# Latent attention's queries in 12 products with transferred rotary parts, and weights loaded four chunks ahead

## The chip, the cores and the metric

The kernel runs on one core of a Trainium2 chip. The metric is the device time of one execution in microseconds. Before the change it is 2968.56 us (median of 3 runs, 2968.51 to 2968.79).

## The reference

A two-layer encoder on 512 tokens of width 1024, all in float32. A layer is a half-step SwiGLU, a mixing block with three kinds of attention, a second half-step SwiGLU, and a gated per-layer input. The change touches the first kind of attention only, multi-head latent attention with 16 heads:

```python
q = (rms_norm(c_q, q_norm) @ w_uq).reshape(b, s, MLA_HEADS, MLA_NOPE + MLA_ROPE)   # 384 -> 16 x (64 + 32)
q_nope = q[..., :MLA_NOPE]
q_rope = apply_rope(q[..., MLA_NOPE:], cos[:, None, :], sin[:, None, :])
kv = (rms_norm(c_kv, kv_norm) @ w_ukv).reshape(b, s, MLA_HEADS, MLA_NOPE + MLA_V)
k_nope, v = kv[..., :MLA_NOPE], kv[..., MLA_NOPE:]
k_rope = apply_rope(k_rope, cos, sin)                       # one for all heads
logits = (einsum('bqhd,bkhd->bhqk', qn, k_nope) + einsum('bqhr,bkr->bhqk', qr, k_rope)) * 96 ** -0.5
```

`apply_rope` splits the 32 numbers into halves x1 and x2 of 16 and gives [x1 cos - x2 sin, x2 cos + x1 sin], here called the turned part. The 64 numbers without rotation are a head's own part.

## The kernel before, in words

**Arithmetic.** Each float32 matrix is split into a high part, cast to a reduced format (fp32r), and a low part, the difference. A product takes three matmuls: high by high, low by high, high by low (`mm3`, L224 is the matmul's line). `split` (L235, L236) makes the parts of an activation: a cast on ScalarE, a subtraction on VectorE.

**Tiles.** Activations lie as tiles of 128 features by 512 tokens. They come from one ring of 62 tiles (`SLOTS`). A product goes to a PSUM bank; of the eight banks three ("a") serve projections and five ("s") the heads' logits and outputs.

**Weights.** All weights are laid out on the host as chunks of 128 x 1024 in the order of use (`_chunk`). `Weights.get` (L128) names a chunk, orders the split of chunks up to two ahead (`SPLIT_AHEAD`), and the load of chunks up to five ahead (`LOAD_AHEAD`, L72). Loads go out on SyncE's queue (L88) into four raw buffers. A chunk is cast on ScalarE (L101), and its low part is made by VectorE (L107) or, in the heads' stage (`by_load`, from L1192), by a negated copy on ScalarE (L104) and an accumulating transfer from the raw buffer that GpSimd issues (L105). The raw buffer is free after that. The split parts have three buffers.

**The mixing block** (`mix`) projects the normalised input to the query latent (three tiles, `cq`), the key and value latent (two tiles, `ckv`) and the rotary key. The key tiles `KA` exist three times for two heads each (`KSETS` = 3): one half of such a tile holds the head's own 64 key rows, the other half 64 rows with the 32 turned key rows twice. Then 40 heads follow each other: 16 latent, 8 differential, 16 windowed. A head's steps are logits (`Mla.logits`, L1001), softmax, transposes, values.

**The order of the work.** Each head's own work is written out in order. The projections that later heads need stand in a queue (`Filler`, L136), sorted by the head at which they are due; `pace` works out how many matmuls per head are to be done, over the whole queue ahead, and `pump` takes that many between a head's steps. What a head needs is forced beforehand (`need`). Pair j (`mla_pair`, L844, the queries and own keys of heads 2j and 2j+1) may start at head 2(j-2), when the key tiles of pair j-3 are free, and is due before head 2j. Pair 0 and the first values are forced before head 0 (L1190). The framework's scheduler then orders each engine's instructions; every engine, SyncE among them, works through its own list in order.

**A pair before the change.** The queries of each head take a product of their own of 128 rows: 64 own rows, the 32 rotary rows, and the same 32 with their halves exchanged. One VectorE multiplication by a table (`trig`, L850) scales the own rows, multiplies the rotary rows by cosine and the exchanged ones by sine. The tile is split. The two products of the rotary rows are added only in the logits' matmul, where both meet the same turned key rows. A pair is thus 9 + 9 matmuls for the queries and 6 for the keys (24 units in the queue), and four tiles of the ring stay until its heads are done.

Of the kernel before, what the change touches and what calls it, by code (L numbers as in the profile page):

```python
# [12 lines left out]
F32 = mybir.dt.float32  # L13
F32R = mybir.dt.float32r
AF = mybir.ActivationFunctionType
ALU = mybir.AluOpType
# [4 lines left out]
P = 128  # L21
D = 1024
KT = D // P
T = 512
# [4 lines left out]
NH = 16  # L29
NHD = 8  # L30
QL = 384
KVL = 256
SCALE_A = 96 ** -0.5
# [34 lines left out]
class Weights:  # L68

    LOAD_AHEAD = 5  # L72
    SPLIT_AHEAD = 2

    def __init__(self, nc, pool, wall):
# [52 lines left out]
    def get(self, *keys):  # L128
        first = self.claim(*keys)[0]
        self.halve(first + max(1 + self.SPLIT_AHEAD, len(keys)))  # L130
        self.load(first + 1 + self.LOAD_AHEAD)
        out = [self.parts.pop(first + i) for i in range(len(keys))]
# [50 lines left out]
def encoder_kernel(ctx: ExitStack, tc: tile.TileContext, ins, out):  # L183
    nc = tc.nc
# [22 lines left out]
    def S(name, dt=F32):  # L207
        return sb.tile([P, 512], dt, tag="slot", name=name, bufs=SLOTS)
# [4 lines left out]
    turn = [0]  # L213

    def PS(name, kind=None):


        if kind is None:
            kind = CYCLE[turn[0] % len(CYCLE)]
            turn[0] += 1  # L220
        return psp.tile([P, 512], F32, tag="ps" + kind, name=name, bufs=BANKS[kind])
# [4 lines left out]
    def mm3(ps, lh, ll, rh, rl, start, stop):  # L226
        mm(ps, lh, rh, start, False)
        mm(ps, ll, rh, False, False)
        mm(ps, lh, rl, False, stop)

    def split(src, name, tile=None):

        tile = tile or S
        hi, lo = tile(name + "h", F32R), tile(name + "l", F32R)
        nc.scalar.copy(hi, src)  # L235
        nc.vector.tensor_sub(lo, src, hi.bitcast(F32))  # L236
        return hi, lo
# [12 lines left out]
    t = S("one")  # L250
# [11 lines left out]
    for l in range(L):  # L262
        for i, at in enumerate((S_F1, S_F2)):
            s = slice(l * 8 + 4 * i, l * 8 + 4 * i + 4)
# [147 lines left out]
    def proj(ps, w, z, i0=0, n=KT, cols=P):  # L412

        wh, wl = w
        for k in range(n):
            c = slice(i0 + k * cols, i0 + k * cols + cols)
            mm3(ps, wh[:, c], wl[:, c], z[k][0], z[k][1], k == 0, k == n - 1)
            if side:
                side.popleft()()
            yield 3  # L420
# [301 lines left out]
    def mix(l, prep, p2):  # L722
        name = f"m{l}"
# [3 lines left out]
        def kept(nm, dt=F32):  # L727
            return stage.tile([P, 512], dt, tag="kept", name=f"{name}{nm}", bufs=17)
# [16 lines left out]
        for d in range(KT):  # L745
            if d % 4 == 0:
                w = W.get(("ple_proj", l, d // 4))
            ps = PS(f"{name}pp{d // 4}{d % 4}")
# [12 lines left out]
        trig = [kept(f"trig{i}") for i in range(3)]  # L761
# [45 lines left out]
        cq, ckv, got = end_q(), [], {}  # L807
# [13 lines left out]
                ckv.extend(end_kv())  # L821

        merged = [None] * KT

        def mla_v(g):
            wh, wl = W.get(("mla_v", l, g))
            vs = [S(f"{name}va{g}_{tb}", F32R) for tb in range(TB)]
            for tb in range(TB):
                ps = PS(f"{name}va{g}_{tb}", "a")[:, 0:256]
                ts = slice(tb * P, (tb + 1) * P)  # L830
                for k in range(2):
                    w = slice(k * 256, (k + 1) * 256)
                    mm(ps, ckv[k][0][:, ts], wh[:, w], k == 0, False)
                    mm(ps, ckv[k][1][:, ts], wh[:, w], False, False)
                    mm(ps, ckv[k][0][:, ts], wl[:, w], False, k == 1)

                v = vs[tb].rearrange("p (g x c) -> p g x c", x=4, c=64)
                src = ps.rearrange("p (g e c) -> p g e c", e=2, c=64)
                nc.scalar.copy(v[:, :, 0::3, :], src)
                nc.vector.tensor_sub(v[:, :, 1:3, :], src, v[:, :, 0::3, :].bitcast(F32))  # L840
                yield 3
            got["va", g] = vs

        def mla_pair(j):  # L844
            wh, wl = W.get(("mla_pair", l, j))
            for e in range(2):
                ps = PS(f"{name}qa{j}{e}", "a")
                yield from proj(ps, (wh, wl), cq, i0=e * 384, n=3)
                t = S(f"{name}qa{j}{e}")
                nc.vector.tensor_mul(t, ps, trig[e])  # L850
                got["qa", 2 * j + e] = split(t, f"{name}qa{j}{e}")
            ps = PS(f"{name}kap{j}", "a")
            yield from proj(ps, (wh, wl), ckv, i0=768, n=2)
            for e in range(2):
                r = slice(0, 64) if e == 0 else slice(64, 128)
                kh, kl = KA[j % KSETS][e]
                nc.scalar.copy(kh[r], ps[r])
                nc.vector.tensor_sub(kl[r], ps[r], kh[r].bitcast(F32))

        halves = (slice(0, 64), slice(64, 128))  # L860

        def q_pair(key, at, j):

# [305 lines left out]


        A0, C0, B0, END = 0, NH, NH + NHD, 2 * NH + NHD
        work = [(A0 + 2 * j - 1, ("pair", j), 24, mla_pair(j)) for j in range(8)]
        work += [(A0 + 4 * g, ("va", g), 12, mla_v(g)) for g in range(4)]
        work += [(A0 + 2 * j + 1, ("ga", j), 24, gate("ga", C_GA, j)) for j in range(2, 8)]
        for j in range(8):
# [150 lines left out]
    for l in range(L):  # L1326
# [9 lines left out]
        ffn(l, "ffn1", prep, pm, hooks)  # L1336
        close_stage()
        sums, outs = mix(l, pm, p2)
        open_stage(True)
        pf = Combos(f"f2_{l}", l, S_F2)  # L1340
# [43 lines left out]
KSETS = 3  # L1384
# [13 lines left out]
def _chunk(ins, key):  # L1398

    kind, c = key[0], None  # L1400
    if kind == "cols":
        _, w, l, i = key
        c = ins[w][l][:, i * P:(i + 1) * P].reshape(KT, P, P)
    elif kind == "in":
        _, l, at = key
        c = ins["w_in"][l][:, at:at + P].reshape(KT, P, P)
    elif kind == "down":
        _, w, l, g, i = key
        rows = ins[w + "_w_down"][l][GROUPS[g].start * P:GROUPS[g].stop * P]
        n = rows.shape[0] // P  # L1410
        c = rows[:, i * (1024 // n):(i + 1) * (1024 // n)].reshape(n, P, 1024 // n)
    elif kind == "out":
        _, l, half, kk = key
        c = ins["w_out"][l][kk * 256:(kk + 1) * 256, half * 512:(half + 1) * 512].reshape(2, P, 512)
    elif kind == "rope":
        w = ins["w_in"][key[1]]
        c = np.concatenate([w[:, C_KR:C_KR + 32], w[:, C_KR + 16:C_KR + 32], w[:, C_KR:C_KR + 16]], axis=1).reshape(KT, P, 64)
    elif kind in ("vb", "vc"):
        l, kk = key[1], key[-1]
        at = C_VB if kind == "vb" else C_VC + key[2] * 256  # L1420
        c = ins["w_in"][l][kk * 512:(kk + 1) * 512, at:at + 256].reshape(4, P, 256)
    elif kind == "mla_v":
        _, l, g = key
        w = ins["mla_w_ukv"][l].reshape(KVL, NH, P)[:, 4 * g:4 * g + 4, 64:]
        c = w.reshape(2, P, 256)
    elif kind == "mla_pair":
        _, l, j = key
        parts = []
        for e in range(2):
            w = ins["mla_w_uq"][l][:, (2 * j + e) * 96:(2 * j + e + 1) * 96]  # L1430
            own, rope = w[:, :64], [w[:, 64:], w[:, 80:], w[:, 64:80]]
            w = np.concatenate([own] + rope if e == 0 else rope + [own], axis=1)
            parts.append(w.reshape(3, P, P))
        w = ins["mla_w_ukv"][l].reshape(KVL, NH, P)[:, 2 * j:2 * j + 2, :64].reshape(KVL, P)
        parts.append(w.reshape(2, P, P))
        c = np.concatenate(parts, axis=0)
    elif kind == "ple_proj":
        _, l, i = key
        c = ins["ple_w_proj"][l][:, i * 512:(i + 1) * 512].reshape(2, P, 4, P).transpose(2, 0, 1, 3).reshape(8, P, P)
    return c.transpose(1, 0, 2).reshape(P, -1)  # L1440


def _trig():
    inv = np.float32(10000.0) ** (-np.arange(0, 32, 2, dtype=np.float32) / np.float32(32))
    ang = np.arange(T, dtype=np.float32)[:, None] * inv.astype(np.float32)[None, :]
    cos, sin = np.cos(ang).T, np.sin(ang).T
    turn = np.concatenate([cos, cos, -sin, sin], axis=0)
    s = np.float32(-SCALE_A)
    own = np.full((64, T), s, np.float32)
    res = np.zeros((3, P, T), np.float32)  # L1450
    res[0] = np.concatenate([own, s * turn])
    res[1] = np.concatenate([s * turn, own])
    res[2, :64] = turn
    return res

# [70 lines left out]
```

## Time and profile before

| | |
|---|---|
| median of 3 runs | 2968.56 us |
| the profiled execution, its time and its span | 2968.8 us, 2967.0 us |
| granted TensorE clock, mean | 0.997 |
| latent heads, layer 0 and layer 1 (first logits to the first differential head) | about 431 to 724 us, 1898 to 2191 us |
| weight loads of 512 KB on SyncE's queue (L88) | 312 |
| accumulating transfers (L105) | 146 |

The profile is one execution. Busy times of the engines overlap. PE is TensorE's matmuls, PEld its weight loads, DVE is VectorE, ACT ScalarE, POOL GpSimd, SP SyncE. A matmul's duration is pipelined, so its cost is read from the distance of starts. Names like `m0qa` mean layer 0, tile qa; `m0A4s` is the logits of layer 0's latent head 4. A name with "q" behind an engine (SPq) is that engine's sequencer, which issues transfers and waits.

### The profile page before, as it was taken

How to read it: one execution, taken by the hardware profiler on the slowest of the kernel's cores; microseconds unless marked ns; L12 is line 12 of the kernel's file. 1: busy time of each engine (PE TensorE's matmuls, PEld its weight loads, DVE VectorE, ACT ScalarE, POOL GpSimd, SP SyncE). 2: the span in 40 equal slices, each digit the busy share in tenths (PEclk: the TensorE clock that was granted, in tenths of full speed). 3: DMA queues.
4: the chain of work that ended last, by engine and by line, in shares of the span. 5: the costliest groups of instructions: out<-in, count | busy, mean ns of one | idle time of the engine just before them, and what ended most of it. 6: DMA issues, size and time to landing. Idle time of an engine off the chain costs nothing.

```text
span 2967.0 us, 45265 instructions
## 1 busy us (share of the span) xinstructions
PE 2917.5 (98%) x16812; PEld 2543.3 (86%) x16812; DVE 2118.4 (71%) x3659; ACT 1786.1 (60%) x3281; POOL 652.2 (22%) x856
## 2 busy tenths in 40 slices
PE   8999999999999999999999999999999999999998
PEld 7999878888888889999889998788888788899996
DVE  7777676645787768778687776765467876687776
ACT  5544457767788855445454454677578888544443
POOL 1131113322333331010211101133223333311103
PEclk9999999999999999999999999999999999999999
DMA  6585435455545557553356634344555465665532
GB/s 220 157 264 142 137 114 135 102 128 143 143 123 129 139 144 211 143 148 105 118 167 165 175 98 165 100 121 109 134 139 148 103 148 133 184 164 149 157 93 85
DMA packets 133932, 421.43 MB, mean 142 GB/s; under 512 B 16174, under 2 KB 18542, under 8 KB 133712
## 3 DMA queue, kind: packets, MB, share of 16 engines
q0 software_dynamic: 53712, 156.01, 26.2%
q1 hardware_dynamic: 78272, 260.64, 25.8%
q8 instruction: 132, 2.16, 0.3%
q10 hardware_dynamic: 1728, 1.90, 0.2%
q14 instruction: 88, 0.72, 0.1%
HBM read 331.39 MB, written 18.94 MB: 118 GB/s over the span
## 4 chain that ended last, share of the span: by engine, by line
PE 86%; ACT 5%; DVE 5%; issue 2%; DMA 1%; POOL 1%; DVEq 0%; ACTq 0%; SPq 0%; POOLq 0%
PE ffn21d L224 4%; PE ffn20d L224 4%; PE ffn10d L224 4%; PE ffn11d L224 4%; PE ple L224 3%; PE wo L224 2%; PE m1ga L224 1%; PE m0ga L224 1%; PE m1qb L224 1%; PE m1qc L224 1%; PE m0qc L224 1%; PE m0qb L224 1%; PE m0vc L224 1%; PE m1vc L224 1%; PE m0gb L224 1%
## 5 line engine op out<-in xcount | busy, mean ns | idle before, releaser
L101 ACT CAST whi<-wraw 128x1024 fp32r<-128x1024 f32 x312 | 326.6, 1050 | 261.7 <-issue 71.2
L107 DVE TENSOR_TENSOR wlo<-wraw,whi 128x1024 fp32r<-128x1024 f32 x166 | 204.1, 1233 | 107.2 <-ACT whi L101 98.8
L105 POOL DMA_DIRECT2D wlo<-wraw x146 | 127.2, 871 | 561.2 <-ACT wlo L104 470.6
L104 ACT ACTIVATE wlo<-whi 128x1024 fp32r<-128x1024 f32 x146 | 154.9, 1061 | 2.1
L554 DVE SCALAR_TENSOR_TENSOR x<-ffn10d,x 128x512 f32<-128x512 f32 x48 | 33.0, 688 | 34.1 <-PE ffn10d L224 34.0
L554 DVE SCALAR_TENSOR_TENSOR wo0h<-ffn11d,wo0h 128x512 f32<-128x512 f32 x48 | 33.0, 687 | 33.4 <-PE ffn11d L224 33.3
L554 DVE SCALAR_TENSOR_TENSOR wo0h<-ffn20d,wo0h 128x512 f32<-128x512 f32 x48 | 32.8, 686 | 31.1 <-PE ffn20d L224 31.1
L554 DVE SCALAR_TENSOR_TENSOR wo1h<-ffn21d,wo1h 128x512 f32<-128x512 f32 x48 | 32.8, 687 | 30.4 <-PE ffn21d L224 30.4
L367 POOL TENSOR_TENSOR f_1sq<-f_1sq,f_1sq 128x512 f32<-128x512 f32 x14 | 21.4, 1526 | 49.3 <-ACT f_1sq L362 49.0
L917 ACT CAST m1kc<-m1kc 64x512 fp32r<-64x512 f32 x32 | 18.6, 582 | 15.0 <-PE m1kc L224 13.5
L917 ACT CAST m0kc<-m0kc 64x512 fp32r<-64x512 f32 x32 | 18.6, 582 | 15.0 <-PE m0kc L224 13.5
L367 POOL TENSOR_TENSOR pg0sq<-pg0sq,pg0sq 128x512 f32<-128x512 f32 x7 | 10.6, 1512 | 71.0 <-ACT pg0sq L362 71.0
L367 POOL TENSOR_TENSOR pg1sq<-pg1sq,pg1sq 128x512 f32<-128x512 f32 x7 | 10.6, 1514 | 69.5 <-ACT pg1sq L362 69.5
L870 DVE SCALAR_TENSOR_TENSOR m1qc<-m1qc,m1qc 64x512 fp32r<-64x512 f32 x16 | 11.0, 689 | 18.9 <-ACT m1qc L869 18.8
L870 DVE SCALAR_TENSOR_TENSOR m0qc<-m0qc,m0qc 64x512 fp32r<-64x512 f32 x16 | 11.0, 688 | 18.9 <-ACT m0qc L869 18.7
L1164 ACT ACT_TABLE_LOAD x16 | 20.5, 1283 | 0.3
L738 POOL DMA_DIRECT2D h_dram<-x x8 | 4.4, 547 | 71.9 <-DVE x L554 71.9
L738 POOL DMA_DIRECT2D h_dram<-wo0h x8 | 4.4, 547 | 71.4 <-DVE wo0h L554 71.4
L938 DVE TENSOR_TENSOR m1vc<-m1vc,m1vc 128x256 fp32r<-128x256 f32 x16 | 6.4, 414 | 14.3 <-ACT m1vc L937 14.2
L938 DVE TENSOR_TENSOR m0vc<-m0vc,m0vc 128x256 fp32r<-128x256 f32 x16 | 6.4, 414 | 14.3 <-ACT m0vc L937 14.2
L869 ACT ACTIVATE m1qc<-m1qc 64x512 fp32r<-64x512 f32 x16 | 9.5, 592 | 10.4 <-PE m1qc L224 9.0
L869 ACT ACTIVATE m0qc<-m0qc 64x512 fp32r<-64x512 f32 x16 | 9.5, 591 | 10.4 <-PE m0qc L224 9.0
(15134 smaller groups left out, 12409.0 us busy)
## 6 DMA issues: line engine op xcount, KB each, us to landing
wraw<-in_wall SPq DMA_DIRECT2D x312, 512.0 KB, 3.4
wlo<-wraw POOLq DMA_DIRECT2D x146, 512.0 KB, 4.7
copies_s<-bias_s POOLq DMA_DIRECT2D x16, 256.0 KB, 9.8
copies_d<-bias_d POOLq DMA_DIRECT2D x8, 512.0 KB, 10.7
h_dram<-x POOLq DMA_DIRECT2D x8, 256.0 KB, 2.7
pp_dram<-m0ppt POOLq DMA_DIRECT2D x8, 256.0 KB, 3.7
wo0h<-h_dram POOLq DMA_DIRECT2D x8, 256.0 KB, 7.0
ple0p<-pp_dram POOLq DMA_DIRECT2D x8, 256.0 KB, 4.4
```

The source lines that it names most:

```text
L101: pin(self.nc.scalar.copy(hi, raw))
L104: self.nc.scalar.activation(lo, hi.bitcast(F32), AF.Copy, scale=-1.0)
L105: self.nc.gpsimd.dma_start(lo.bitcast(F32), raw, accum_op=ALU.add)
L107: self.nc.vector.tensor_tensor(lo, raw, hi.bitcast(F32), op=ALU.subtract)
L224: nc.tensor.matmul(ps, lhsT, rhs, start=start, stop=stop, skip_group_check=True)
L367: self.engine.tensor_tensor(self.acc, self.acc, sq, op=ALU.add)
L554: nc.vector.scalar_tensor_tensor(h[d], ps, 0.5, h[d], op0=ALU.mult, op1=ALU.add)
L869: nc.scalar.activation(qs[e][own], ps[own], AF.Copy, scale=-0.125)
L870: nc.vector.scalar_tensor_tensor(qs[e][other], ps[own], -0.125, qs[e][own].bitcast(F32), op0=ALU.mult, op1=ALU.subtract)
L917: nc.scalar.copy(ks[e][r], ps[own])
L938: nc.vector.tensor_sub(t[:, 256:512], ps, t[:, 0:256].bitcast(F32))
L1164: nc.scalar.activation(r, ss, AF.Sqrt, bias=eps, scale=1.0 / P)
```

## The change

- **Queries.** For every second pair (j even) one product of 128 rows makes the rotary parts of four heads (2j to 2j+3), with the first halves of all four in rows 0 to 63 and the second halves in rows 64 to 127. VectorE multiplies it by cosine, multiplies the exchanged halves by sine, adds, and the result is split. Then 16 transfers on SyncE's queue carry 16 rows of 512 numbers each to the four heads' tiles: into the rotary half of head i's high tile come the 32 turned rows' high part and, below it, their low part, so that this half of a tile holds both.
- Each pair makes one product for the own parts of both heads (instead of two). ScalarE writes an own high part into the head's high tile, VectorE its low part into a low tile `QL`, whose other half is cleared once per layer by GpSimd. There are six such tiles per layer, reused every third pair.
- A pair with j even is 9 + 9 + 6 matmuls (24 units in the queue), one with j odd 9 + 6 (15 units). In a layer there are 12 query products instead of 16.
- The order of columns in the chunks of weights and the trigonometric table follow. The count and size of the chunks stay.
- `LOAD_AHEAD` is 4, not 5.

```diff
-    LOAD_AHEAD = 5
+    LOAD_AHEAD = 4
...
+        QL = [[S(f"{name}ql{s}{e}", F32R) for e in range(2)] for s in range(KSETS)]
+        for s in range(KSETS):
+            for e in range(2):
+                nc.gpsimd.memset(QL[s][e][halves[1 - e]].bitcast(F32), 0.0)
...
         def mla_pair(j):
             wh, wl = W.get(("mla_pair", l, j))
+            at = 0
+            if j % 2 == 0:
+                ps = PS(f"{name}qr{j}", "a")
+                yield from proj(ps, (wh, wl), cq, n=3)
+                at = 384
+                y, z = S(f"{name}qr{j}y"), S(f"{name}qr{j}z")
+                nc.vector.tensor_mul(y, ps, trig[0])
+                for e in range(2):
+                    nc.vector.tensor_mul(z[halves[e]], ps[halves[1 - e]], trig[1][halves[1 - e]])
+                nc.vector.tensor_add(y, y, z)
+                parts = split(y, f"{name}qr{j}")
+                for i in range(4):
+                    q = got["qh", 2 * j + i] = S(f"{name}qh{2 * j + i}", F32R)
+                    for x, part in enumerate(parts):
+                        for b in range(2):
+                            to = halves[1 - i % 2].start + 32 * x + 16 * b
+                            nc.sync.dma_start(q[to:to + 16].bitcast(F32), part[64 * b + 16 * i:64 * b + 16 * i + 16].bitcast(F32))
+            ps = PS(f"{name}qa{j}", "a")
+            yield from proj(ps, (wh, wl), cq, i0=at, n=3)
             for e in range(2):
-                ps = PS(f"{name}qa{j}{e}", "a")
-                yield from proj(ps, (wh, wl), cq, i0=e * 384, n=3)
-                t = S(f"{name}qa{j}{e}")
-                nc.vector.tensor_mul(t, ps, trig[e])
-                got["qa", 2 * j + e] = split(t, f"{name}qa{j}{e}")
+                own = halves[e]
+                qh, ql = got.pop(("qh", 2 * j + e)), QL[j % KSETS][e]
+                nc.scalar.activation(qh[own], ps[own], AF.Copy, scale=-SCALE_A)
+                nc.vector.scalar_tensor_tensor(ql[own], ps[own], -SCALE_A, qh[own].bitcast(F32), op0=ALU.mult, op1=ALU.subtract)
+                got["qa", 2 * j + e] = qh, ql
             ps = PS(f"{name}kap{j}", "a")
-            yield from proj(ps, (wh, wl), ckv, i0=768, n=2)
+            yield from proj(ps, (wh, wl), ckv, i0=at + 384, n=2)
...
-        work = [(A0 + 2 * j - 1, ("pair", j), 24, mla_pair(j)) for j in range(8)]
+        work = [(A0 + 2 * j - 1, ("pair", j), (24, 15)[j % 2], mla_pair(j)) for j in range(8)]
```

More of the change, by code (lines that the diff above doesn't have):

```diff
@@ L823, in mix @@
         merged = [None] * KT
+        halves = (slice(0, 64), slice(64, 128))
+        QL = [[S(f"{name}ql{s}{e}", F32R) for e in range(2)] for s in range(KSETS)]
+        for s in range(KSETS):
+            for e in range(2):
+                nc.gpsimd.memset(QL[s][e][halves[1 - e]].bitcast(F32), 0.0)
         def mla_v(g):
@@ L858, in mla_pair @@
                 nc.vector.tensor_sub(kl[r], ps[r], kh[r].bitcast(F32))
-        halves = (slice(0, 64), slice(64, 128))
         def q_pair(key, at, j):
@@ L1427, in _chunk @@
         _, l, j = key
[L1428 to L1433, printed above, removed]
+        w = ins["mla_w_uq"][l].reshape(QL, NH, 96)
+        parts = [w[:, 2 * j:2 * j + 2, :64].reshape(3, P, P)]
+        if j % 2 == 0:
+            w = w[:, 2 * j:2 * j + 4, 64:].reshape(QL, 4, 2, 16).transpose(0, 2, 1, 3)
+            parts.insert(0, w.reshape(3, P, P))
         w = ins["mla_w_ukv"][l].reshape(KVL, NH, P)[:, 2 * j:2 * j + 2, :64].reshape(KVL, P)
@@ L1448, in _trig @@
     s = np.float32(-SCALE_A)
-    own = np.full((64, T), s, np.float32)
     res = np.zeros((3, P, T), np.float32)
-    res[0] = np.concatenate([own, s * turn])
-    res[1] = np.concatenate([s * turn, own])
+    res[0] = np.tile(s * cos, (8, 1))
+    res[1] = np.concatenate([np.tile(s * sin, (4, 1)), np.tile(-s * sin, (4, 1))])
     res[2, :64] = turn
```

## The prediction

> **What bounds the kernel now.** I read the page first (busy shares, clock, the chain that ended last), then the windows of latent attention, then the rows around its first head, then SyncE's queue.
>
> ```profile
> span 2967.0 us, 45265 instructions
> PE 2917.5 (98%) x16812; PEld 2543.3 (86%) x16812; DVE 2118.4 (71%) x3659; ACT 1786.1 (60%) x3281; POOL 652.2 (22%) x856
> PEclk9999999999999999999999999999999999999999
> PE 86%; ACT 5%; DVE 5%; issue 2%; DMA 1%; POOL 1%; DVEq 0%; ACTq 0%; SPq 0%; POOLq 0%
> ```
>
> TensorE is busy for 98% of the span at full granted clock and carries 86% of the chain; no other engine carries over 5%. Work taken from TensorE therefore shortens the run, unless something it then waits for takes its place. The windows of layer 0 (columns: busy time of PE, PEld, DVE, ACT, POOL, then clock, DMA share, GB/s) are the sixteen latent heads (431 to 724) and the differential heads after them (724 to 950):
>
> ```profile
> 431.00:724.00 293.00, 289.75 (x1530) 245.40 (x1528) 170.29 (x304) 206.03 (x383) 81.97 (x103) 1.00 0.52 126
> 724.00:950.00 226.00, 219.87 (x1189) 186.68 (x1188) 172.48 (x338) 188.44 (x354) 75.95 (x96) 1.00 0.53 131
> ```
>
> TensorE idles 3.3 us in the first and 6.1 us in the second, while VectorE has 123 us and ScalarE 87 us free in the first. The paced projections of these two stages come from one queue (`Filler`), so what a latent projection loses in matmuls is handed on evenly to both; both are bound by TensorE.
>
> **The removed matmuls.** A query product is three 128-row blocks by three matmuls, 9 of 128x512. Today there are 16 per layer (two for each of 8 pairs); after it 12 (8 "own" and 4 "turned"). In two layers 2 x 4 x 9 = 72 matmuls go. The rows (start, duration) show what one costs in a dense run:
>
> ```profile
> L224 PE MATMUL m0qa<-m0cq0h,whi x16: 389/390/504, 423.5 to 567.3; 128*128 128x512 f32 x16
> 418.10 0.39 PE L224 MATMUL m0ga<-m0m0u0h,whi 128*128 128x512 f32 x1
> 423.31 0.39 PE L224 MATMUL m0ga<-m0u7l,whi 128*128 128x512 f32 x1
> 423.54 0.39 PE L224 MATMUL m0qa<-m0cq0h,whi 128*128 128x512 f32 x1
> ```
>
> The first row counts 16 products in a layer. The 0.39 us is a pipelined duration; the cost is the distance of starts. From 418.10 (first of a gate's 24) to 423.54 (the next product's first) it is 5.44 / 24 = 0.2267 us. So 72 x 0.2267 = 16.3 us leave TensorE, 8.2 per layer. The logits keep their three matmuls per block.
>
> **The new chain to the first head.** This is where the price is. Today a product is multiplied by the table, cast, subtracted, and the head starts:
>
> ```profile
> 429.06 0.69 DVE L236 TENSOR_TENSOR m0ckv1l<-m0ckv,m0ckv1h 128x512 fp32r<-128x512 f32 x1
> 429.66 0.69 DVE L850 TENSOR_TENSOR m0qa<-m0qa,m0trig 128x512 f32<-128x512 f32 x1
> 430.38 0.62 ACT L235 CAST m0qa00h<-m0qa 128x512 fp32r<-128x512 f32 x1 [1.59 <-DVE m0qa L850]
> 431.03 0.69 DVE L236 TENSOR_TENSOR m0qa00l<-m0qa,m0qa00h 128x512 fp32r<-128x512 f32 x1 [0.69 <-ACT m0qa00h L235]
> 431.72 0.50 PE L224 MATMUL m0A0s<-m0ka00h,m0qa00h 128*128 128x512 f32 x1
> ```
>
> Head 0's first logits start at 431.72, the moment its low part ends. The turned product takes the first place, with VectorE free for it at 429.66. It needs four VectorE steps instead of one (a whole multiply, two half ones, an add); a half-height tile costs as much as a whole one (the 64x512 rows below), and steps follow each other every 0.60 us (429.06, 429.66). They start at 429.66, 430.26, 430.86, 431.46; the add ends at 432.15, the cast at 432.80, the low part at 433.52. Then come the transfers, on SyncE:
>
> ```profile
> L870 DVE SCALAR_TENSOR_TENSOR m0qc<-m0qc,m0qc x16: 684/688/694, 588.5 to 839.9; 64x512 fp32r<-64x512 f32 x16
> L869 ACT ACTIVATE m0qc<-m0qc 64x512 fp32r<-64x512 f32 x16 | 9.5, 591 | 10.4 <-PE m0qc L224 9.0 <-DVE m0qc L870 1.2
> L88 SPq DMA_DIRECT2D wraw<-in_wall x312: 327/328/1175, 1.2 to 2919.5; - x156
> DMA to landing us min/median/max: 3.1/3.4/14.0
> L1370 SPq DMA_DIRECT2D out<-out x8: 332/340/446, 2958.2 to 2962.6; - x8
> DMA to landing us min/median/max: 1.7/2.0/2.6
> ```
>
> No transfer inside SBUF of 32 KB stands in this trace. The nearest rows are the output stores of 128 KB (0.34 us to issue, landed after 2.0, at most 2.6) and the weight loads of 512 KB (0.33 us, 3.4). I take 0.33 and 2.0, the smallest transfer. A head needs four, two of high parts and two of low. Issued head by head, the second low one goes out at 433.52 + 0.66 = 434.2 and lands at 436.2: head 0 is 4.5 us later than today. If all eight high ones go first, the last needed one goes out at 432.80 + 10 x 0.33 = 436.1 and lands, at 2.6, at 438.7: 7.0 later. I take 5.
>
> The eight stores went out 0.6 us apart on average (4.4 us over seven steps) and landed after 2.0 each, so their waits overlapped; I let the four pieces overlap too.
>
> **What covers it.** TensorE meets the wait after the pair's 24 matmuls, as many as today, at 431.05:
>
> ```profile
> 431.05 0.71 PE m0va L224 x6
> 431.76 1.17 PE m0A0s L224 x4
> 432.93 0.71 PE m0va L224 x6
> 433.65 1.84 PE m0A0s L224 x8
> 435.49 0.45 PE m0A1s L224 x2
> 435.94 1.43 PE m0va L224 x12
> 437.37 4.11 PE m0qa L224 x18
> ```
>
> The 24 value matmuls (2.85 us) and pair 1 (now 15 matmuls, 3.4 us) need no query, 6.25 us against the 5.2 from 431.05 to 436.2. But each product needs one of three PSUM banks, emptied by VectorE and ScalarE, and here VectorE is full:
>
> ```profile
> 420.00:430.00 10.00, 9.13 (x38) 6.53 (x37) 10.00 (x14) 6.22 (x9) 0.00 (x0) 1.00 0.16 50
> 430.00:440.00 10.00, 10.00 (x56) 8.58 (x55) 8.91 (x16) 6.94 (x13) 0.00 (x0) 1.00 0.35 109
> ```
>
> VectorE is busy 10.00 of 10 us, then 8.91, and gets three more steps. The bound is nothing lost (all covered) to 5 per layer and more (no cover). I take half the lateness, 2.5 per layer, 5.0 in two.
>
> **Later pairs.** Turned products exist for pairs 0, 2, 4, 6. Pair 2 is ready long before its head:
>
> ```profile
> L236 DVE TENSOR_TENSOR m0qa20l<-m0qa,m0qa20h x1: 1159/1159/1159, 450.2 to 450.2; 128x512 fp32r<-128x512 f32 x1
> L224 PE MATMUL m0A4s<-m0ka20h,m0qa20h x4: 389/391/396, 489.2 to 495.7; 128*128 128x512 f32 x4
> ```
>
> The split starts at 450.2, the head at 489.2: 39 us cover a chain that is 5 to 7 us longer. Nothing. Without that cover it would cost as much as at head 0, 2.5 a pair, 15 for the six.
>
> **Engines beside TensorE.** Per four heads VectorE goes from eight steps of 0.69 (5.5 us) to nine (6.2), ScalarE from four casts of 0.62 (2.5) to one and four of 0.59 (3.0): over eight such groups 5.5 and 4 us, inside idle time. Six clears of the zero halves run on GpSimd:
>
> ```profile
> L251 POOL MEMSET one<- x1: 538/538/538, 4.6 to 4.6; 128x512 f32 x1
> 440.58 0.89 POOL L105 DMA_DIRECT2D wlo<-wraw x1 [61.93 <-ACT wlo L104]
> ```
>
> 6 x 0.54 = 3.2 us in a queue that idles 61.9 us before the first head's work. Nothing; uncovered, 3.2 a layer. The tile ring (62) holds six zero-padded low parts and up to eight high ones, against twelve today: two more, no cost taken.
>
> **SyncE's queue and loading four ahead.** The transfers wait on SyncE for the split, and the loads behind wait with them.
>
> ```profile
> SPq L88 <- DMA wlo<-wraw: 1221.6, 146, 23.5
> SPq L88 <- DVE wlo L107: 639.6, 129, 21.0
> 393.26 203.14 SPq L88 DMA_DIRECT2D wraw<-in_wall  x27
> 445.23 0.33 SPq L88 DMA_DIRECT2D wraw<-in_wall  x1
> ```
>
> SyncE waits 1861 us in all for one of the four raw buffers; the buffers time the loads, not the count ahead. Twenty-seven loads in 203 us make 7.5 us a chunk. A load goes when the chunk four before it is split, three chunks before its own cast: 22.5 - 3.4 = 19 us of margin. Sixteen issues (5.3 us) fit; so does a load given out one chunk later. Cost nothing; with no margin, 8 x 5.3 = 42 us.
>
> **Sum.** The profiled execution took 2968.8 us, its span 2967.0 with 1.8 around it, 0.24 above the median of 2968.56. 2968.8 - 16.3 + 5.0 = 2957.5; on the median 2957.3.
>
> **Rivals.** *All covered*: pair 1 and the values fill the wait, as their 6.25 us allow: 2968.56 - 16.3 = 2952.3. Against it stands VectorE's full window. *Nothing covered*: head 0 is late by 5 to 7 us in each layer and TensorE waits it all, 10 to 14 us: 2962.3 to 2966.3, mostly no change by my bound; the full VectorE speaks for it, the plentiful ready work against. *Slower*: head 0's transfers stand in SyncE's queue behind the load that waits for its buffer until 445.23. Then four issues end at 446.9, landing at 448.9, 17.9 us after 431.05; less 6.25 of cover, 11.6 a layer, 23.2 in all: 2975.5. It passes the bound if the landing comes after 448.4. That this load comes one place later in the program now, and is ready only 12 us after the split, speaks against. *Transfers in series*: if head 0's four pieces paid their 2.0 us one after the other from 432.80 on, they would land at 440.8, 9.1 late; with half of that uncovered the two layers lose 9.1: 2961.4. The stores' overlap speaks against. (The Trainium skill, DMA: Bandwidth & Descriptors, "Rules for kernel authors", says to coalesce many small transfers, because under 64 KB one pays mostly overhead; this change cuts 128 pieces of 32 KB. By that rule the fixed part is paid per piece; no run here shows pieces of this size, and the stores agree only in that 128 KB took 2.0 us where 512 KB took 3.4.) *The matmuls were not the bound*: TensorE then waits for split weights or ScalarE (188 of 226 us busy in the differential heads) what it saves, about 2966 to 2969; the chain's 86% speaks against.
>
> **How the numbers follow.** About 0.2%, 5.9 us, can be told from no change: faster is below 2962.6, slower above 2974.5. Forecast 0.40, all covered 0.25, nothing covered 0.18, transfers in series 0.05, matmuls not the bound 0.05, slower 0.07. Of "nothing covered" 0.02 lies below 2962.6: faster 0.40 + 0.25 + 0.05 + 0.02 = 0.72, same 0.21, slower 0.07. Range: 2951 (all covered, less about 1 of TensorE's 9.4 idle us shifting with the new order) to 2967 (nothing covered at 7 a layer); about 0.12 lie above and 0.06 below.
>
> **What would show it.** Right: 36 query matmuls fewer in each layer, head 0's first logits about 5 us after the pair's last matmul, a few us of TensorE idle there, later heads waiting for no transfer, casts of weights not later. Wrong: waits of TensorE on the transfers at heads 4, 8 or 12, waits of casts on loads, or a stall over 10 us before head 0.

## The result and the profile after

The changed kernel takes 2996.19 us (median of 4 runs, 2995.72 to 2997.39) against 2968.68 for the kernel before beside it: a ratio of 1.0091 [1.0079, 1.0104], 27.5 us slower. The prediction was 2957.3, 2951 to 2967, faster. It was wrong in sign and size. The medians below leave out the one slow execution, of a_nocopy at 4812.27 us (with it that run's median is 2969.43).

The page of the changed kernel: span, busy shares, the chain that ended last.

```profile
span 2994.8 us, 45484 instructions
...
PE 2917.6 (97%) x16740; PEld 2540.1 (85%) x16740; DVE 2124.5 (71%) x3667; ACT 1792.2 (60%) x3289; POOL 651.9 (22%) x868
...
PE 84%; DVE 6%; ACT 5%; issue 2%; DMA 1%; SPq 1%; POOL 0%; DVEq 0%; ACTq 0%; POOLq 0%
```

The 72 matmuls are gone (16812 to 16740), yet TensorE's busy time is what it was, 2917.6 us: those that are left were busy longer. VectorE has gained a point of the chain, and SyncE's sequencer (SPq) appears in it with 1%. The windows of layer 0, with the columns of before (PE, PEld, DVE, ACT, POOL busy, clock, DMA share, GB/s):

```profile
431.00:724.00 293.00, 274.51 (x1417) 231.33 (x1416) 161.67 (x284) 197.65 (x366) 73.35 (x96) 0.97 0.52 125
724.00:950.00 226.00, 220.88 (x1180) 186.46 (x1180) 171.80 (x330) 187.47 (x345) 72.91 (x90) 1.00 0.54 133
```

The loss lies in the latent heads. In the same 293 us TensorE now idles 18.5 us instead of 3.3, 15.2 more in a layer, 30 in two, and the granted clock's mean is 0.97 instead of 1.00. What TensorE waited for there (us in total, times, longest):

```profile
PE m0ga L224 <- DVE m0va L846: 5.4, 1, 5.4
PE m0va L224 <- DVE m0ka01l L885: 4.2, 2, 3.5
PE m0va L224 <- DVE m0ka21l L885: 3.4, 1, 3.4
...
```

Three stalls of over 3 us (the second row holds two waits, one of 3.5), and none of them names a transfer. The first and the last in time are followed up below; the middle one, at the values behind pair 2, comes back in the run c_cover.

**Head 0.** VectorE's list at the first pair:

```profile
430.62 0.68 DVE L859 TENSOR_TENSOR m0qr0y<-m0qr,m0trig 128x512 f32<-128x512 f32 x1
431.31 1.39 DVE L861 TENSOR_TENSOR m0qr0z<-m0qr,m0trig 64x512 f32<-64x512 f32 x2
432.73 0.68 DVE L885 TENSOR_TENSOR m0ka00l<-m0kap,m0ka00h 64x512 fp32r<-64x512 f32 x1
433.34 0.67 DVE L862 TENSOR_TENSOR m0qr0y<-m0qr0y,m0qr0z 128x512 f32<-128x512 f32 x1
433.94 1.21 DVE L107 TENSOR_TENSOR wlo<-wraw,whi 128x1024 fp32r<-128x1024 f32 x1
435.08 0.68 DVE L236 TENSOR_TENSOR m0qr0l<-m0qr0y,m0qr0h 128x512 fp32r<-128x512 f32 x1
...
436.38 0.69 DVE L885 TENSOR_TENSOR m0ka01l<-m0kap,m0ka01h 64x512 fp32r<-64x512 f32 x1
```

The steps do follow each other every 0.6 to 0.7 us, but a key's low part and a chunk of weights (1.21 us) stand between the turned product's own. The first step also begins 1.0 us later than the 429.66 of the prediction. The low part starts at 435.08; the prediction had it end at 433.52. SyncE's queue then, and TensorE's rows at the same place:

```profile
434.80 1.42 SPq L870 DMA_DIRECT2D m0qh<-m0qr0h  x2
436.28 1.21 SPq L870 DMA_DIRECT2D m0qh<-m0qr0l  x2
...
443.85 1.22 SPq L870 DMA_DIRECT2D m0qh<-m0qr0l  x2
445.11 0.58 SPq L88 DMA_DIRECT2D wraw<-in_wall  x1
```

```profile
433.45 0.28 PE L224 MATMUL m0va<-wlo,m0ckv1h 128*128 128x256 f32 x1
437.22 0.55 PE L224 MATMUL m0va<-whi,m0ckv0h 128*128 128x256 f32 x1 [3.49 <-DVE m0ka01l L885]
...
439.92 0.63 PE L224 MATMUL m0A0s<-m0ka00h,m0qh 128*128 128x512 f32 x1
440.35 0.63 PE L224 MATMUL m0A0s<-m0ka00h,m0ql 128*128 128x512 f32 x1
...
442.11 0.39 PE L224 MATMUL m0A0s<-m0ka00h,m0qh 128*128 128x512 f32 x1
442.34 0.39 PE L224 MATMUL m0A0s<-m0ka00h,m0ql 128*128 128x512 f32 x1
```

The first logits come at 439.92, 8.2 us later than before. But TensorE stands still earlier, 3.49 us between 433.45 and 437.22, and for another reason: the next values product needs a PSUM bank, and the last step that empties one (`m0ka01l`) is late in VectorE's list. The values that were to cover the transfers were themselves held up. When they end, the logits follow without a wait: the last of head 0's four pieces went out at about 436.9 and landed some 2.0 us later, a microsecond before the logits. Without the stall TensorE would have come to the logits near 435.0 (an estimate: twelve values matmuls more at 0.12 us), before that piece. So the two waits lie over each other, and the bank's was the one that showed. Behind the stall the same kind of matmul starts every 0.43 us (439.92, 440.35) instead of 0.23 (442.11, 442.34). The clock column of the windows shows it:

```profile
430.00:440.00 10.00, 5.72 (x28) 4.89 (x27) 7.62 (x12) 4.65 (x8) 0.00 (x0) 0.74 0.36 115
...
460.00:470.00 10.00, 7.29 (x28) 6.48 (x29) 6.21 (x12) 7.66 (x16) 2.25 (x3) 0.66 0.59 143
...
570.00:580.00 10.00, 9.24 (x31) 7.19 (x32) 2.31 (x6) 4.99 (x9) 2.25 (x3) 0.76 0.52 119
```

After each of the three long stalls the granted clock falls, and a stretch that looks 92% busy (570 to 580) holds 31 matmuls where before it held 54 (16 of those narrower, of 128 columns). (The Trainium skill, TensorE: Matmul & The Clock Gate, "Why this matters for your kernels", says to leave no gap over about 3 us between bursts of matmuls, or the clock drops to half. The trace agrees: 3.49 us idle, then a distance of 0.43 for 0.23.) It is no safe limit here, though: in the run a_nocopy below 1.85 us idle at the same place were followed by the same distance of 0.43, and in c_banks 2.66 us idle, up to 511.48, by the full clock.

**A tile that is handed on.** The third stall is the longest. The rows of the transfers' line give the time of one issue (min/median/max, ns) and who waited for them:

```profile
L870 SPq DMA_DIRECT2D m0qh<-m0qr0h x8: 507/548/587, 434.8 to 443.2; - x8
L870 SPq DMA_DIRECT2D m0qh<-m0qr0l x8: 574/587/587, 436.3 to 444.5; - x8
...
who waited for it (us, times):
  ACT m0A8p L1038: 5.4, 1
  ACT m1A8p L1038: 4.8, 1
  ACT m0A3pth L983: 4.7, 1
...
DMA to landing us min/median/max: 1.9/2.0/5.3
```

No head's logits: softmax tiles of heads that have nothing to do with the turned rows. ScalarE and TensorE at the first of them:

```profile
569.21 0.69 ACT L1038 ACTIVATE m0A8p<-m0A8s,m0A8m 128x512 f32<-128x512 f32 x1 [5.40 <-DMA m0qh<-m0qr6h]
```

```profile
565.08 0.28 PE L224 MATMUL m0va<-wlo,m0ckv1h 128*128 128x256 f32 x1
570.76 0.79 PE L224 MATMUL m0ga<-m0m0u0h,whi 128*128 128x512 f32 x1 [5.41 <-DVE m0va L846]
```

The exponential of head 8 is to be written to the ring tile that held `m0qr6h`. That tile is free only when the last of the eight transfers that read it has landed, some 12 us after the first was issued. ScalarE waits 5.4 us, the casts of the values behind it wait, VectorE's subtraction waits for these, and TensorE for the bank: three engines stop for a tile that nobody needs in a hurry.

### The profile page after: what moved, and what is told of

The parts are those of the page before. It is cut to its first block, busy times and chain, and to the rows that moved or that the text cites. A ratio compares the mean times of both kernels' runs of the same rounds, so it can differ in the third digit from the quotient of the medians.

```text
span 2994.8 us, 45484 instructions
## 1 busy us (share of the span) xinstructions
PE 2917.6 (97%) x16740; PEld 2540.1 (85%) x16740; DVE 2124.5 (71%) x3667; ACT 1792.2 (60%) x3289; POOL 651.9 (22%) x868
## 3 DMA queue, kind: packets, MB, share of 16 engines
q1 hardware_dynamic: 82368, 264.84, 26.2%
## 4 chain that ended last, share of the span: by engine, by line
PE 84%; DVE 6%; ACT 5%; issue 2%; DMA 1%; SPq 1%; POOL 0%; DVEq 0%; ACTq 0%; POOLq 0%
PE ffn21d L224 4%; PE ffn20d L224 4%; PE ffn10d L224 4%; PE ffn11d L224 4%; PE ple L224 3%; PE wo L224 2%; PE m1gb L224 1%; PE m0gb L224 1%; PE m1qb L224 1%; PE m0qb L224 1%; PE m1qc L224 1%; PE m0qc L224 1%; PE m0vc L224 1%; PE m1vc L224 1%; ACT whi L101 1%
## 5 line engine op out<-in xcount | busy, mean ns | idle before, releaser
L942 ACT CAST m1kc<-m1kc 64x512 fp32r<-64x512 f32 x32 | 18.6, 581 | 13.0 <-PE m1kc L224 12.6
L942 ACT CAST m0kc<-m0kc 64x512 fp32r<-64x512 f32 x32 | 18.6, 581 | 13.0 <-PE m0kc L224 12.6
L224 PE MATMUL m0va<-whi,m0ckv0h 128*128 128x256 f32 x16 | 6.1, 383 | 11.1 <-DVE m0ka01l L885 4.2
```

What stands on the lines that cost most here:

```text
L224: nc.tensor.matmul(ps, lhsT, rhs, start=start, stop=stop, skip_group_check=True)
L942: nc.scalar.copy(ks[e][r], ps[own])
```

## The experiments

The theory was that the transfers cost it all: their late landing at head 0 and the ring tiles that they hold. The rivals: the steps of the turned product in the queues of VectorE and ScalarE, which keep PSUM banks from TensorE, and the loading four ahead. Every time below is a median, with its ratio to the kernel before on the same chip (2968.8 to 2969.5). The kernel before itself differs by up to 0.7 us between the chips.

**a_ahead5, b_ahead4: the count of loads.** The changed kernel with five ahead, the kernel before with four.

```diff
-    LOAD_AHEAD = 4
+    LOAD_AHEAD = 5
```

> The changed kernel with loads five ahead again. Theory (transfers): the loss comes from the sixteen transfers per turned product, which take 0.63 us each on SyncE instead of 0.33 and hold what they read; the loads are not late, so this stays at 2996 within 6 us. Rival (loads): loading four ahead makes weights late, so it returns to about 2970. Rival (banks): the longer emptying of PSUM banks by VectorE and ScalarE is the loss; 2996 too.

> The kernel before with loads four ahead and nothing else. Theory (transfers) and rival (banks): no change, 2968.6 within 3 us, since the four raw buffers time the loads. Rival (loads): slower by 10 us or more.

2996.57 (1.009 [1.0074, 1.0107]) and 2968.66 (1.0 [0.9991, 1.0009]). The count is worth nothing either way.

**a_nocopy: no transfers.**

```diff
-                    for x, part in enumerate(parts):
-                        for b in range(2):
-                            to = halves[1 - i % 2].start + 32 * x + 16 * b
-                            nc.sync.dma_start(...)
+                    nc.gpsimd.memset(q[halves[1 - i % 2]].bitcast(F32), 0.0)
```

> The changed kernel without its 128 transfers: the rotary half of each head's high tile is cleared by GpSimd instead, so the rotary part is left out of the logits; the turned product, its VectorE steps and its split remain. Theory (transfers): most of the loss goes, 2955 to 2970. Rival (banks): the bank waits remain, 2980 or more. Rival (loads): 2996.

2968.97 (0.9999 [0.9989, 1.0009]). The rotary parts are left out of this kernel's logits. The transfers, with what hangs on them, cost 27.2 us. But without them the kernel is only level with the one before: 16.3 us of matmuls fewer, and nothing to show for it. A second cost of that size was left to find.

**a_tiles: tiles of their own for the split parts.**

```diff
+        def turned(nm, dt):
+            return sb.tile([P, 512], dt, tag="turned", name=nm, bufs=2)
...
-                parts = split(y, f"{name}qr{j}")
+                parts = split(y, f"{name}qr{j}", turned)
...
-SLOTS = 62
+SLOTS = 60
```

> The changed kernel with the split parts of the turned product, which the transfers read, in two tiles of their own, and a ring of 60 tiles instead of 62. Theory (transfers, by the tiles they hold): the waits of ScalarE for transfers before the softmax of head 8 (5.7 us of idle TensorE) and the transposes of head 3 go, with the slow clock after the first; 2975 to 2987. Theory (transfers, by the delay of head 0 alone): no change, 2996. Rival (banks): no change, 2996.

2983.56 (1.0048 [1.0033, 1.0063]): 12.6 us less. That is net, since the stall at head 0 has grown from 3.5 to 4.8 us in this kernel (the first row). The list under "who waited for it" is empty in this kernel, and the landing is what it was:

```profile
PE m0va L224 <- DVE m0ql L880: 5.1, 2, 4.8
...
who waited for it (us, times):
busy tenths in 40 slices 0000000000000000000000000000000000000000
DMA to landing us min/median/max: 1.9/2.0/5.7
```

**c_cover, b_cover: work ahead of head 0.** A gate product (24 matmuls on one bank) runs between pair 0 and the values, in the kernel with own tiles and, as a control, in the kernel before.

```diff
-        work += [... for j in range(2, 8)]
+        work += [... for j in range(3, 8)]
...
-        fill.need(("pair", 0), ("va", 0))
+        fill.need(("pair", 0))
+        run(gate("ga", C_GA, 2))
+        fill.done.add(("ga", 2))
+        fill.need(("va", 0))
```

> The run a_tiles (2983.6 us) with the gate product of pair 2 (24 matmuls in one PSUM bank, 5.4 us) put between pair 0 and the first values, so that TensorE has work while the turned product goes through VectorE and SyncE. Theory (head 0's transfers wait uncovered, 5 us idle and a slow clock after it in each layer): most of the 14 us between a_tiles and a_nocopy goes, 2968 to 2975. Rival (banks): PSUM banks stay occupied just as long and the next waits are only moved, 2980 or more.

> Control: the kernel before with the same gate product moved ahead of the first values. Both theories: head 0 does not wait there today, so no gain, 2968.7 within 4 us. If it gains over 8 us, the cover has a worth of its own that the change has nothing to do with.

2969.93 (1.0002 [0.9993, 1.0012]), 13.6 less than a_tiles; the control 2967.26 (0.9993 [0.9984, 1.0002]), 1.7 less than the kernel before beside it. The uncovered wait at head 0, in two layers, cost 12 to 14 us. With the tiles that makes 26.2, near the 27.2 of a_nocopy, and it stops at the same place, level with before. But the two are not the same thing. What the gate product covers at head 0 is the bank's wait first: in no trace of these kernels does TensorE wait over 0.7 us for a transfer to a head. And a_nocopy, without any transfer, still stands at head 0 (below).

What TensorE still waits for in c_cover, layer 0:

```profile
PE m0va L224 <- DVE m0ka21l L888: 2.7, 1, 2.7
PE m0va L224 <- DVE m0ka11l L888: 1.8, 1, 1.8
PE m0va L224 <- DVE m0ka01l L888: 1.6, 1, 1.6
```

Each time a values product stands behind a pair with a turned product, and waits for the last step that empties that pair's banks.

**c_banks, c_pool.** c_banks copies the two query products out of PSUM by one ScalarE step each, and works from the copy; c_pool issues the low parts' 64 transfers on GpSimd's queue. Both start from a_tiles.

```diff
+                raw = S(f"{name}qr{j}p")
+                nc.scalar.copy(raw, ps)
+                ps = raw
```

```diff
-                            nc.sync.dma_start(...)
+                            (nc.sync, nc.gpsimd)[x].dma_start(...)
```

> The run a_tiles with each query product copied out of PSUM by one ScalarE step, so that its bank is free after 0.6 us of work; the turning and splitting steps read the copy in SBUF. It costs one more ScalarE step per product. Theory (banks): TensorE's waits for banks behind VectorE (5.1, 3.0, 2.1, 1.9 us per layer in a_tiles) go, 2960 to 2972. Theory (head 0's transfers): head 0 gets its transfers a step later, the wait stays, 2982 to 2988.

> The run a_tiles with the low part's transfers (64 of 128) on GpSimd's queue. Theory (SyncE's 0.63 us per issue delays head 0): the four of head 0 go out by two queues, its logits 1 us earlier, 2979 to 2983. Rival (GpSimd has its own queue of accumulating transfers and softmax scalings, which now wait for the split): slower than 2984.

c_banks: 2993.63 (1.008 [1.0063, 1.0097]), a miss, 10 us slower than a_tiles. Two banks come free early, but the pair's key steps now come later:

```profile
PE m0va L224 <- DVE m0ka21l L893: 4.3, 1, 4.3
```

4.3 us instead of the 2.7 of a_tiles and c_cover at the same place: the same step ends the wait, and the lists ahead of it have grown by the copies. That fits a cost of the lists' length rather than of any one bank; no run shows it apart. c_pool: 2981.72 (1.0041 [1.0026, 1.0055]), as expected, 1.8 less.

**e_order, b_order, e_defer, e_all: the order of the steps.** From c_cover. e_order makes the values due a head later and behind the gate of the same due time; b_order does so in b_cover. e_defer puts the turned product's sum, split and transfers behind the emptying of the pair's other banks (pairs 2, 4, 6). e_all has both, and c_pool's queues.

```diff
-        work += [(A0 + 4 * g, ("va", g), 12, mla_v(g)) for g in range(4)]
...
+        work += [(A0 + 4 * g + (g > 0), ("va", g), 12, mla_v(g)) for g in range(4)]
```

```diff
-                nc.vector.tensor_add(y, y, z)
-                parts = split(y, f"{name}qr{j}", turned)
...
+                def turn():
+                    nc.vector.tensor_add(y, y, z)
+                    parts = split(y, f"{name}qr{j}", turned)
...
+            if j % 2 == 0 and j > 0:
+                turn()
```

> The kernel with own tiles and the gate product at the start (2969.9), and the value products of heads 4, 8 and 12 due one head later and behind the gate of the same due time, so that they no longer stand right behind a pair with a turned product, whose three PSUM banks take nine VectorE steps to empty. Theory (what is left of the lost 16.3 us is TensorE waiting for these banks, 3.0, 2.05 and 1.9 us between starts in each layer at 458, 500 and 552 us, and the slowed clock behind them): 12 to 16 us less, 2954 to 2959. Rival (the banks are waited for at whatever product stands there, so the wait moves and stays): 2966 to 2972.

> Control: the same two moves, gate and values, in the kernel before (with the gate alone 2967.3). There the two waits at the same products are 0.9 and 1.5 us between starts in a layer, so both theories allow 0 to 4 us: 2963 to 2968. If it gains as much as the changed kernel does, the order of the work and not the change is what was found.

> The kernel with own tiles and the gate at the start (2969.9), and for pairs 2, 4 and 6 the sum, the split and the transfers of the turned product put behind the steps that empty the pair's other two banks. Two of nine VectorE steps, some 1.4 us, then no longer stand ahead of the emptying, at three places in each of two layers. Theory (banks emptied by VectorE): about 8 us less, 2960 to 2965. Rival (the wait is for something else): 2968 to 2972.

> The two moves of the last expectations together (values later, the turned product's own steps behind the emptying), and the low parts' transfers on GpSimd's queue, which alone was worth 1.8. Theory: at least what the later values alone give, less 0 to 4 more: 2951 to 2957, faster than the kernel before by more than can be mistaken, and so near the 2952 that the 72 removed matmuls leave. Rival: no lower than 2964.

e_order 2971.97 (1.0004 [0.9995, 1.0013]): a miss, the rival's value. b_order 2964.2 (0.9984 [0.9975, 0.9993]). e_defer 2966.86 (0.9988 [0.998, 0.9997]), 3 less where 8 were expected. e_all 2956.69 (0.9953 [0.9941, 0.9966]), 13 less, as the theory had it. One move brought nothing, the other little, all three together nearly everything: the bank theory as it stood did not explain that. In e_order a wait for exponentials had taken the bank's place at pair 4, and one of the same length at pair 6:

```profile
PE m0A3t L983 <- ACT m0A4p L1041: 2.1, 1, 2.1
```

**a_nosteps: without the steps.** From a_nocopy; besides the transfers it leaves out the two half multiplications, the sum and the split of the turned product.

```diff
-                for e in range(2):
-                    nc.vector.tensor_mul(z[halves[e]], ps[halves[1 - e]], trig[1][halves[1 - e]])
-                nc.vector.tensor_add(y, y, z)
-                parts = split(y, f"{name}qr{j}")
```

> The changed kernel without the transfers and, beyond that, without four of the five VectorE steps and the one cast with which the turned product is summed and split: it is only multiplied once by the table, and the heads' rotary halves are cleared on GpSimd instead. Left out: the queries' rotary parts. The matmuls are those of the changed kernel. Without the transfers alone it took 2969.4. Theory (these steps, in the queues of VectorE and ScalarE ahead of what TensorE needs next, swallow the 16.3 us of the removed matmuls): 2952 to 2958. Rival (the matmuls of this stage did not bound): 2964 to 2969.

2949.81 (0.9935 [0.9922, 0.9947]), 19.2 less than a_nocopy with the same matmuls, 20.1 less than c_cover, and 19.1 less than the kernel before. The queries' rotary parts are left out here too. So TensorE did bound this stage, the 16.3 us are there, and 4 VectorE steps and one cast per turned product, 32 and 8 steps in the whole run, swallow them. The latent windows of a_nocopy and a_nosteps:

```profile
431.00:724.00 293.00, 284.26 (x1486) 239.90 (x1485) 174.06 (x308) 209.43 (x388) 84.60 (x115) 0.99 0.52 125
```

```profile
431.00:724.00 293.00, 290.65 (x1530) 245.13 (x1529) 169.41 (x306) 214.71 (x398) 85.40 (x116) 1.00 0.54 130
```

TensorE idles 8.7 us in the one and 2.4 in the other. VectorE, whose steps make the difference, is busy 59% and 58% of the time: the share hardly tells of it.

The waits by which the steps reach TensorE are not the same in every kernel. In c_cover they are the three for banks above, 6.1 us a layer, 12 of the 20.1. In a_nocopy hardly any wait is for a bank behind VectorE (0.8, 0.3 and 0.2 us); the longest end with ScalarE:

```profile
PE m0A0s L224 <- ACT m0qh L873: 1.9, 1, 1.9
PE m0A0t L977 <- ACT m0A1p L1035: 1.6, 1, 1.6
```

The first is head 0: six values matmuls, then nothing until a step on ScalarE that stands behind the turned product's cast, and half clock behind it (0.72 from 430 to 440, against 1.00 in a_nosteps). The second is pair 2. ScalarE waits there for the turned product's sum, with the exponentials of head 1 behind the cast:

```profile
454.76 0.62 ACT L235 CAST m0qr2h<-m0qr2y 128x512 fp32r<-128x512 f32 x1 [2.27 <-DVE m0qr2y L862]
...
457.43 0.68 ACT L1035 ACTIVATE m0A1p<-m0A1s,m0A1m 128x512 f32<-128x512 f32 x1
```

So the same steps reach TensorE by two roads, a bank that is emptied late or an exponential that is made late. How the 20 us divide between the single steps was not taken apart.

**e_od, e_op, e_dp, e_p: the three moves of e_all apart.** o: values later; d: turned steps behind; p: half the transfers on GpSimd. All from c_cover.

> The gate at the start, the values later and the turned product's own steps behind the emptying, all transfers on SyncE. Each of the two moves alone left a wait of 2 us a pair at the same place, for ScalarE's exponentials (values later) or for a bank (steps behind), and brought +2 and -3 us. Theory (the two waits stand one behind the other, so that only both moves together show the gain): 2956 to 2961. Rival (GpSimd's queue for half the transfers made the gain of 13): 2965 to 2970.

> The gate at the start, the values later and the low parts' transfers on GpSimd, the turned product's steps where they were. Theory (the two moves in the program make the gain, the queue 2 us): 2967 to 2972. Rival (the queue makes it): 2957 to 2962.

> The gate at the start, the turned product's own steps behind the emptying, the low parts' transfers on GpSimd, the values where they were. Theory (both moves are needed): 2963 to 2967. Rival (the queue makes the gain): 2957 to 2962.

> The gate at the start and the low parts' transfers on GpSimd, nothing else moved: what is missing to tell the three moves apart (none 2969.9; values later 2972.0; turned steps behind 2966.9; both 2969.1; the queue with values later 2957.1, with turned steps behind 2963.1, with both 2956.7). Theory now (half the transfers off SyncE is worth something by itself where head 0 is covered, and the later values add to it): 2961 to 2966. Rival (it works with the later values only): 2967 to 2970.

| | transfers on SyncE | low parts' on GpSimd |
|---|---|---|
| neither move | 2969.93 (c_cover) | 2965.54, 0.9987 [0.9978, 0.9996] (e_p) |
| turned steps behind | 2966.86 (e_defer) | 2963.07, 0.9979 [0.997, 0.9987] (e_dp) |
| values later | 2971.97 (e_order) | 2957.08, 0.9957 [0.9945, 0.997] (e_op) |
| both | 2969.14, 1.0 [0.9991, 1.0009] (e_od) | 2956.69 (e_all) |

The theory that both moves in the program are needed fell: e_od was expected at 2956 to 2961, and e_op came in where the rival, the queue, had it. e_dp and e_p lie where their theories had them. GpSimd's queue is worth 4 us by itself, 15 with the values later, and with these two the deferred steps add nothing that can be told. How the columns come to differ with the values later is seen at ScalarE in e_order and e_op, after the last cast of pair 4's keys. First e_order:

```profile
500.25 0.58 ACT L887 CAST m0ka11h<-m0kap 64x512 fp32r<-64x512 f32 x1
503.73 1.05 ACT L101 CAST whi<-wraw 128x1024 fp32r<-128x1024 f32 x1 [2.90 <-PE m0ga L224]
...
506.37 0.69 ACT L1041 ACTIVATE m0A4p<-m0A4s,m0A4m 128x512 f32<-128x512 f32 x1
```

Then e_op:

```profile
498.57 0.58 ACT L887 CAST m0ka11h<-m0kap 64x512 fp32r<-64x512 f32 x1
...
499.79 0.69 ACT L1041 ACTIVATE m0A4p<-m0A4s,m0A4m 128x512 f32<-128x512 f32 x1
...
503.37 1.05 ACT L101 CAST whi<-wraw 128x1024 fp32r<-128x1024 f32 x1
```

The same instructions stand in another order. In e_order a cast of weights stands ahead of head 4's exponentials, and it must wait 2.90 us until TensorE's gate product has let go of a split buffer; the exponentials, ready by then, wait behind it. In e_op they stand ahead. Nobody wrote that: the kernels differ in the queue of 64 transfers, and the framework's scheduler laid ScalarE's list out differently. How much of the 15 us comes from the lists and how much from SyncE's shorter queue was not told apart.

**e_gps: two steps off VectorE.** From e_op; for pairs 2, 4 and 6 the turned product's sum and low part are made by GpSimd.

```diff
-                nc.vector.tensor_add(y, y, z)
-                parts = split(y, f"{name}qr{j}", turned)
+                eng = nc.gpsimd if j else nc.vector
+                eng.tensor_tensor(y, y, z, op=ALU.add)
+                parts = [turned(f"{name}qr{j}{x}", F32R) for x in "hl"]
+                nc.scalar.copy(parts[0], y)
+                eng.tensor_tensor(parts[1], y, parts[0].bitcast(F32), op=ALU.subtract)
```

> The gate at the start, values later and the low parts' transfers on GpSimd (2957.1), and for pairs 2, 4 and 6 the turned product's sum and its low part on GpSimd, not VectorE: two of five VectorE steps fewer. Theory (the turned product's steps in VectorE's queue are what still parts it from the 2949.8 without them): 2952 to 2955. Rival (GpSimd's 1.5 us steps, and the weights' transfers queued behind them, take it back): 2957 to 2962.

2955.03 (0.9952 [0.9938, 0.9966]), at the edge of what the theory allowed and not to be told from e_op. This version, e_all and e_op beat both kernels: about 13 us under the one before, some 40 under the changed one. The order alone, without the change, brings the kernel before to 2964.2 (b_order); the change is worth 7 to 9 us beyond that, about half of its removed matmuls (the control has no such transfers, so it can't share what their queue is worth).

## Why the prediction was wrong, point by point

- **"72 x 0.2267 = 16.3 us leave TensorE": right.** The count is right, and a_nosteps lies 19.1 us under the kernel before: the 16.3, and 2.8 that may come from the VectorE and ScalarE steps it has fewer.
- **"I take half the lateness, 2.5 per layer, 5.0 in two": the place was right, the wait and the size were not.** It cost 13.6 (c_cover, from a stall that had grown in a_tiles). The logits were 8.2 late and not 5: the steps do not stand back to back (the split's low part began 2.3 us later than forecast, with a later first step, a chunk of weights and a key's part ahead of it), issues came 0.63 apart and not 0.33, and 18 values matmuls instead of 6 went first, most of them at half clock. TensorE did not wait for the transfers at all: the cover failed in the way the prediction mentioned and then halved, since the values waited for VectorE's banks. The clock that falls after a stall was in no term.
- **"The tile ring ... two more, no cost taken": wrong, 12.6 us** (a_tiles). The prediction counted the heads' tiles, left out the turned product's own (`y`, `z` and the two split parts), and did not ask how long each is held. A tile that a queue of transfers reads is held for as long as that queue runs.
- **"Later pairs ... Nothing" and "Engines beside TensorE ... inside idle time": wrong, 19.2 us without transfers** (a_nosteps against a_nocopy), 20.1 with them (against c_cover). This is the step that failed worst: a term put at nothing because the steps fit into idle time alone swallows the saving, and the 26 us of the two points above come on top. No later head waited for its queries; the 39 us of cover were there. But VectorE's nine steps stand in one list. Before, a query's bank was free after one step of VectorE; now the turned product's is free after three and the own product's after two and two of ScalarE's. Summed over four heads that is one step more, and the sum was all that the prediction looked at; at the even pair it is a run of nine where each pair had six, and what TensorE needs next, a bank or an exponential, waits behind it (c_cover and a_nocopy above).
- **Issue of 0.33 us, landing of 2.0.** The landing was right, 2.0 in the median. An issue took 0.55 to 0.59 us, 0.63 from one to the next, so 16 take 10 us and not 5.3. The stores taken for it have four times the bytes and are cheaper to issue; bytes were the wrong likeness. Shape is not all of it either: the load of 512 KB that goes out right behind the sixteen pieces, at 445.11, took 0.58 too, where loads take 0.33 in the median. (The Trainium skill, DMA: Bandwidth & Descriptors, "Rules for kernel authors", says to coalesce many small transfers, since under 64 KB one pays mostly overhead. The trace agrees: 0.55 to 0.59 us of issue for each piece of 32 KB, and a landing of 2.0 as with stores of four times the bytes.)
- **SyncE's loads and loading four ahead at nothing: right** (a_ahead5, b_ahead4; casts of weights wait 3.9 us for loads in the changed kernel, 3.5 in the one before).
- **The rivals.** "Nothing covered" named the right place, at 10 to 14 us a run, which is what c_cover measured, but it had TensorE wait there for the transfers: the size agreed by luck, and its sum held nothing for tiles and steps. "Slower" had the transfers behind the waiting load; they went out at 434.80 and the load at 445.11, in the other order. A slower outcome was given 0.07, with that one mechanism; the two that decided, tiles and the list of steps, were in the text as costs of nothing.

The terms do not add up exactly: -16.3, +13.6, +12.6 and +19.2 make 29.1, against the 27.5 measured. They overlap: the 13.6 and the 19.2 both hold the stall at head 0 that a_nocopy has and a_nosteps has not. Read along one path, from a_nosteps at 2949.81 it is 20.1 up to c_cover, 13.6 to a_tiles and 12.6 to the changed kernel; in another order the shares would differ.

## What to carry to other kernels

The engine that bounds the kernel gets its saving only if the other engines' lists are not longer at the place where it goes next; look at the longest run of steps ahead of what it needs there, not at the busy share. Count for every transfer how long it holds the tile that it reads, and give such tiles a buffer of their own. If the framework lays out each engine's list, a change of queue can reorder engines that it does not touch, so compare the lists and take a control with the same move in the old kernel.

## What the runs showed of the hardware

- A transfer of 16 rows of 2 KB inside SBUF took SyncE's sequencer 0.55 to 0.59 us to issue in the median and landed 2.0 us later; a load of 128 rows with sixteen times the bytes took 0.33, but 0.58 directly behind sixteen such pieces.
- After 3.49 us idle TensorE's starts lay 0.43 us apart for a matmul that takes 0.23, and the slow stretch lasted about 4 us (437.22 to 441.6). In a_nocopy 1.85 us idle sufficed; in c_banks 2.66 us idle did not slow it. In a run at 0.992 mean clock such stretches are easily overlooked: the page's clock line shows 9 in every slice.
